# Latent norms moved into the projections, and a pair's split spread over three jobs, in a two-layer diffusion block

## The chip, the cores and the metric

The kernel runs on one core of a Trainium2 chip. A core has five engines, each with its own queue of instructions: TensorE (PE in the profile; its weight loads are a row of their own, PEld), VectorE (DVE), ScalarE (ACT), GpSimd (POOL) and SyncE (SP, which here only issues DMAs). Engines wait for each other through semaphores. Matmuls write to PSUM, in banks of 128 partitions by 512 fp32 numbers; everything else lies in SBUF. The metric is device time in microseconds for one execution, taken several times; less is better.

## What is computed

Two layers of a diffusion transformer over 512 latent tokens and 256 context tokens (768 columns in the kernel), 1024 features, all in fp32. Layer 0 runs two kinds of attention heads side by side, layer 1 another kind; both end in a SwiGLU block. The change touches the first layer's heads:

```python
def mla_heads(p_lat, p_ctx, ...):            # 8 latent-attention heads
    def queries(p, rotate):
        q = rms_norm(p[..., :256], q_norm) @ w_q_up          # query latents, 256
        ...
    def keys(p, rotate):
        c_kv = rms_norm(p[..., 256:384], kv_norm)            # key/value latent, 128
        k_rope = p[..., 384:]                                # key rope part, 32
        ...
def na_heads(q, k, v, qc, kc, vc, rel_bias, ctx_out):        # 8 neighbourhood heads
    s_lat = einsum(q, k_blk) * scale + col_bias              # keys near the query on the grid
    s_ctx = einsum(q, kc) * scale
    p = softmax(concatenate([s_ctx, s_lat], axis=-1))
    ...
def rms_norm(x, gain):
    return x * rsqrt(mean(x * x, axis=-1) + EPS) * gain
```

The two `rms_norm` of the latents are "the latent norms". The inputs of both kinds of heads come from one projection of the modulated tokens.

## The kernel before

**Arithmetic.** A product of fp32 matrices is made of three matmuls on rounded halves: with a = ah + al and b = bh + bl, the kernel adds ah·bh, ah·bl and al·bh (L324, L325, L326). So every operand must be *split*: the high half is a cast (on ACT or another engine), the low half a subtraction (on DVE or POOL). Weights are split the same way after they are loaded: wh by ACT (L311), wl by DVE or POOL (L312).

**Layer 0, projections.** Features lie on partitions, tokens along the free dimension, so that one projection gives a tile of 128 features by 768 tokens. `projections()` first makes queries and keys of the first two pairs of neighbourhood heads (head pairs 0 and 1), then goes through the string `AFTER = "012k5678"`: 0 and 1 are the two tiles of the query latents, 2 the key/value latent, k the key's rope part, 5 to 8 the raw queries and keys of pairs 2 and 3. Beside it runs background work: the modulation vectors of later stages. Their weights are loaded by DMAs that SP issues in order, multiplied on DVE and POOL (L241, L258) and summed on ACT (L259); DVE adds the parts (L261, L262). Other modulation vectors come from matmuls with the conditioning vector (L191), picked out by four small matmuls (L195).

**Layer 0, neighbourhood attention.** `na_jobs()` yields, for each of the four head pairs, three jobs (context queries, and two halves of the latent queries). A job computes scores (L768, PE, into PSUM), adds the bias and takes the running row minimum (L546, DVE; its row carries the name CUSTOM_DVE_ANT or ISA), exponentiates (L542, ACT), transposes the probabilities (L483, PE), copies and splits them out of PSUM (L474 DVE, L475 ACT), and weighs the values (L536, PE). The bias of a latent score tile is a pair of tiles loaded per head (`nb_tiles`, tag nb, two buffers).

**Side work.** Work that the attention does not need at once is put into a queue of generators, `side_work`, which `attend` advances by `step()` while it emits a job. `STEPS[0]` says how many steps a job of each pair takes, `PATTERN` at which four places of a job. `ORDER = ("2", "n3", "m", "")` says what is queued at each pair: during pair 0 the split of pair 2, during pair 1 the latent norms and the split of pair 3, during pair 2 the preparation of the latent attention (`mla_prepare`). Side work is emitted at a lower priority (`LOWER`). The order on each engine is then set by a scheduler that simulates the engines' times and takes the ready instruction of highest priority.

**What the change touches.** `split_pair` (its casts and subtractions stand at L723, L735, L744) moves a pair's raw queries and keys into split halves; `RK` says which engine casts the keys' high halves of pairs 2 and 3 (0 ACT, 1 POOL, 2 DVE). `gained` is the latent norms: squares on POOL (L962), their sum on DVE (L966), 12 column sums by matmuls with ones on PE (L969), two roots on ACT (L972, with a load of the table that holds the root, and afterwards another of the table that holds the exponential), reciprocals (L973), then a step later the transposes that spread the results over the partitions (L453), ACT's copy of them out of PSUM (L981), the multiplication by gain and root on DVE (L984) and the split (L348, L349). `latent_operands` puts the rope part of the keys into the operand of the first two latent heads by four copies (L1101), two for each. `mla_prepare` loads and splits three weights, their low halves on POOL (L312).

**PSUM.** The general ring `PG()` hands out banks by the string "stsdtsd" (tags s, t, d), one place further at each call; `PQ()` always hands out a d bank.

## Time and profile before

| what | before |
|---|---|
| time, median of 3 runs (least to most) | 1573.08 us (1572.73 to 1574.07) |
| time of the profiled execution | 1573.01 us |
| its span, first to last instruction | 1571.2 us |
| mean granted TensorE clock | 0.992 of full |
| PE busy | 1524.4 us, 97% |
| DVE busy | 1180.6 us, 75% |
| ACT busy | 804.4 us, 51% |
| POOL busy | 282.3 us, 18% |

The profiled execution is as long as the runs; 1.8 us of it lie outside the span. The busy shares are averages over many stages. The edited work lies between 100 and 262 us from the span's start: the projections end at 185, the neighbourhood attention follows. In the rows below, a line starts with L and the line's number, then come engine and operation (or engine first, in a timeline), what is written and read, the tile's size and how often. Numbers of buffers are left out of names: `pss`, `pst`, `psd` are PSUM banks with tag s, t, d; `b`, `p`, `st`, `nb`, `wr`, `wh`, `wl`, `sm` are SBUF tiles by tag. In a row of a timeline the number behind the start is a duration, and [0.67 <-ACT p L193] says that the engine sat idle for 0.67 us before it until ACT at L193 had written p.

### The profile page before, as it was taken

How to read it: one execution, taken by the hardware profiler on the slowest of the kernel's cores; microseconds unless marked ns; L12 is line 12 of the kernel's file. 1: busy time of each engine (PE TensorE's matmuls, PEld its weight loads, DVE VectorE, ACT ScalarE, POOL GpSimd, SP SyncE). 2: the span in 40 equal slices, each digit the busy share in tenths (PEclk: the TensorE clock that was granted, in tenths of full speed). 3: DMA queues.
4: the chain of work that ended last, by engine and by line, in shares of the span. 5: the costliest groups of instructions: out<-in, count | busy, mean ns of one | idle time of the engine just before them, and what ended most of it. 6: DMA issues, size and time to landing. Idle time of an engine off the chain costs nothing.

```text
span 1571.2 us, 26600 instructions
## 1 busy us (share of the span) xinstructions
PE 1524.4 (97%) x9942; PEld 1355.7 (86%) x9942; DVE 1180.6 (75%) x2351; ACT 804.4 (51%) x1638; POOL 282.3 (18%) x316
## 2 busy tenths in 40 slices
PE   6999889999999999999999999999999999999998
PEld 4787767887998999999999999877789998899997
DVE  5494878657588588895877776888877778688686
ACT  5354587777376234242433345557866445354453
POOL 0173724233010010111112110382002000000000
PEclk9999999999999999999999999999999999999999
DMA  9457242102462465656566665130016133233232
GB/s 343 153 170 235 77 132 76 44 11 95 164 224 88 148 207 174 224 156 241 179 214 245 205 242 194 40 117 32 1 29 187 45 103 130 89 100 124 86 101 88
DMA packets 82129, 216.63 MB, mean 138 GB/s; under 512 B 10832, under 2 KB 18896, under 8 KB 82000
## 3 DMA queue, kind: packets, MB, share of 16 engines
q1 hardware_dynamic: 66640, 163.02, 32.4%
q0 software_dynamic: 13056, 48.77, 9.1%
q10 hardware_dynamic: 2304, 3.15, 0.5%
q8 instruction: 78, 1.28, 0.3%
q14 instruction: 51, 0.42, 0.1%
HBM read 187.10 MB, written 23.07 MB: 134 GB/s over the span
## 4 chain that ended last, share of the span: by engine, by line
PE 74%; DVE 6%; issue 4%; DMA 3%; ACT 2%; POOL 0%; DVEq 0%; POOLq 0%; ACTq 0%; SPq 0%
PE pso L536 5%; PE pss L1408 4%; PE pss L1406 4%; PE pss L1407 4%; PE pss L324 3%; PE pss L325 3%; PE psd L324 3%; PE pss L326 3%; PE psd L1408 3%; PE psd L325 3%; PE psd L1406 3%; PE psd L326 3%; PE psd L1407 3%; PE pss L768 3%; PE pst L483 2%
## 5 line engine op out<-in xcount | busy, mean ns | idle before, releaser
L311 ACT CAST wh<-wr 128x512 fp32r<-128x512 f32 (+2 forms) x139 | 105.9, 776 | 197.4 <-DMA wr<-in_w_dn_dram 39.9
L312 DVE TENSOR_TENSOR wl<-wr,wh 128x512 fp32r<-128x512 f32 (+2 forms) x136 | 127.5, 944 | 71.2 <-ACT wh L311 70.6
L542 ACT ACTIVATE p<-p,sm 128x512 f32<-128x512 f32 (+3 forms) x144 | 105.1, 730 | 34.0 <-DVE sm L546 33.3
L1408 PE MATMUL pss<-b,wl 128*128 128x384 f32 (+1 forms) x302 | 93.8, 311 | 1.9 <-DVE wl L1394 1.9
L1406 PE MATMUL pss<-b,wh 128*128 128x384 f32 (+1 forms) x302 | 93.6, 310 | 0.0
L1407 PE MATMUL pss<-b,wh 128*128 128x384 f32 (+1 forms) x302 | 93.5, 310 | 0.0
L536 PE MATMUL pso<-ph,b 128*64 128x256 f32 (+1 forms) x400 | 78.3, 354 | 2.3 <-DVE ph L474 2.1
L1406 PE MATMUL psd<-b,wh 128*128 128x384 f32 (+1 forms) x256 | 79.8, 312 | 0.6 <-ACT p L1456 0.6
L1407 PE MATMUL psd<-b,wh 128*128 128x384 f32 (+1 forms) x256 | 79.8, 312 | 0.0
L1408 PE MATMUL psd<-b,wl 128*128 128x384 f32 (+1 forms) x256 | 79.2, 311 | 0.0
L325 PE MATMUL psd<-b,wh 128*128 128x512 f32 (+3 forms) x224 | 78.4, 350 | 0.0
L536 PE MATMUL pso<-pl,b 128*64 128x256 f32 (+1 forms) x400 | 77.7, 353 | 0.2 <-ACT pl L475 0.2
L768 PE MATMUL pss<-st,st 128*128 128x512 f32 (+2 forms) x264 | 69.8, 379 | 7.8 <-DVE sm L546 7.6
L324 PE MATMUL pss<-st,wh 128*128 128x256 f32 (+2 forms) x226 | 75.5, 334 | 0.6 <-ACT st L1393 0.6
L326 PE MATMUL pss<-st,wl 128*128 128x256 f32 (+2 forms) x226 | 75.4, 334 | 0.0
L324 PE MATMUL psd<-b,wh 128*128 128x512 f32 (+3 forms) x208 | 74.9, 360 | 0.1
L326 PE MATMUL psd<-b,wl 128*128 128x512 f32 (+3 forms) x208 | 73.4, 354 | 0.0
L325 PE MATMUL pss<-b,wh 128*128 128x256 f32 (+3 forms) x223 | 70.5, 318 | 0.0
L1393 ACT CAST wh<-ph 128x512 fp32r<-128x512 f32 x80 | 46.4, 620 | 33.4 <-DVE ph L1428 14.3
L1393 ACT CAST wh<-pl 128x512 fp32r<-128x512 f32 x80 | 45.9, 619 | 30.0 <-PE psd L1407 12.2
L1393 ACT CAST wh<-wr 128x1024 fp32r<-128x1024 f32 x40 | 42.0, 1050 | 37.0 <-PE pst L325 10.1
L483 PE MATMUL pst<-ident_r,p 128*128 128x128 f32 x346 | 58.2, 277 | 1.7 <-DVE ph L474 0.6
(615 smaller groups left out, 5315.5 us busy)
## 6 DMA issues: line engine op xcount, KB each, us to landing
wr<-in_w_gu_dram SPq DMA_DIRECT2D x88, 512.0 KB, 4.1
wr<-in_w_out_dram SPq DMA_DIRECT2D x32, 512.0 KB, 3.5
wr<-in_w_dn_dram SPq DMA_DIRECT2D x64, 256.0 KB, 2.8
p<-home SPq DMA_DIRECT2D x40, 384.0 KB, 5.0
home<-p POOLq DMA_DIRECT2D x40, 384.0 KB, 5.2
nb<-in_mod_w_dram POOLq DMA_DIRECT2D x48, 256.0 KB, 3.9
rope<-in_mod_w_dram POOLq DMA_DIRECT2D x24, 512.0 KB, 4.1
wr<-in_w_in_dram SPq DMA_DIRECT2D x21, 512.0 KB, 4.9
```

The source lines that it names most:

```text
L311: S.copy(h, r)
L312: (G if eng else V).tensor_tensor(lo, r, f(h), op=ALU.subtract)
L324: PE.matmul(o, wh[:, k], mh[:, c], start=first and k == 0, stop=False)
L325: PE.matmul(o, wh[:, k], ml[:, c], start=False, stop=False)
L326: PE.matmul(o, wl[:, k], mh[:, c], start=False, stop=last and k == n - 1)
L536: ins = PE.matmul(o[64 * i : 64 * i + 64, c], v(kt), t, start=n == 0, stop=n == len(moving[i]) - 1)
L542: S.activation(p[:, c], p[:, c], AF.Exp, bias=nm, scale=-1.0, accum_out=dn)
L768: PE.matmul(o, x, k, start=i == 0, stop=i == 1)
L1393: S.copy(h, t)
L1406: PE.matmul(o, wh, xh, start=first and k == 0, stop=False, skip_group_check=not first)
L1407: PE.matmul(o, wh, xl, start=False, stop=False, skip_group_check=not first)
L1408: PE.matmul(o, wl, xh, start=False, stop=k == 3, skip_group_check=not first)
```

## The change

The latent norms are cut in three. `latent_squares` is called inside the projections, right behind the second and third latent tile: ACT squares them, DVE adds the two of the query latents; the results go into tiles of tags nb and p. `latent_roots` is called behind projection "5": the ones-matmuls into a bank of the general ring, both roots at once, the reciprocal into a tile that stays, `latent_cols`. Behind projection "7" ACT computes one exponential whose value nobody uses, so that the exponential's table is loaded there. What is left of `gained` spreads `latent_cols` over partitions by transposes, and DVE multiplies straight out of PSUM, in pieces of 512 and 256 columns; ACT's copies and the tile they wrote are gone. The keys' high halves of pair 2 are cast by ACT instead of DVE. `STEPS[0][0]` goes from 2 to 1, so that the split of pair 2 takes one step a job. The four rope copies of `latent_operands` go from DVE to POOL. Since the roots take a bank of the general ring, all later users of it get the next place of the string.

```diff
--- before.py
+++ after.py
@@ -61,7 +61,8 @@
 C1 = 0
 VP = 0
 TURN1, MANY = (0,), 0
-RK, RQ, RL, SQ = (2, 0), (0, 0), (0, 0), 1
+RK, RQ, RL = (0,0), (0, 0), (0, 0)
+ROOTS_AT, EXP_AT = '5', '7'
 PT = (("p", "p", "p", "wr"), ("p", "p", "p", "wr"), ("p",))
 COPY = ("vva", "vvva", "vva")
 L3 = 50
@@ -72,7 +73,7 @@
 PATTERN = ("fbsfbsfbbsfs",) * 3
 BG = ((0, 0, 0, 0, 0), (2, 3), (0, 0), (0, 0))
 FIRST = 2000
-STEPS = ((2, 3, 4, 4), 5, 3)
+STEPS = ((1,3,4,4), 5, 3)
 HALVES = (slice(0, 256), slice(256, 512))
 SWAP8 = [(i // 16) * 16 + (i % 16 + 8) % 16 for i in range(32)]
 SWAP16 = [(i + 16) % 32 for i in range(32)]
@@ -949,41 +950,39 @@
 
         return use
 
-    def gained(groups):
-
-        d, m = PQ(), NT // P
-        n = m * len(groups)
-        col = T("sm", [P, 6, 2]).rearrange("p a b -> p (a b)")[:, :n]
-        for i, (tiles, _) in enumerate(groups):
-            acc = None
-            for t in tiles:
-                s = B()
-                if SQ:
-                    G.tensor_tensor(s, t, t, op=ALU.mult)
-                else:
-                    S.activation(s, t, AF.Square)
-                if acc is not None:
-                    V.tensor_tensor(s, s, acc, op=ALU.add)
-                acc = s
+    latent_cols = T("latent_cols", [P, 12])
+
+    def latent_squares(tiles, tag):
+
+        ss = [B(tag=tag) for _ in tiles]
+        for s, t in zip(ss, tiles):
+            S.activation(s, t, AF.Square)
+        for s in ss[1:]:
+            V.tensor_tensor(ss[0], ss[0], s, op=ALU.add)
+        return ss[0]
+
+    def latent_roots(accs):
+
+        d, m = PG(), NT // P
+        for i, (acc, _) in enumerate(accs):
             for j in range(m):
                 PE.matmul(d[:, i * m + j : i * m + j + 1], acc[:, j * P : (j + 1) * P], ones[:, :1], start=True, stop=True)
-        for i, (tiles, _) in enumerate(groups):
+        for i, (_, n) in enumerate(accs):
             c = slice(i * m, i * m + m)
-            S.activation(col[:, c], d[:, c], AF.Sqrt, bias=eps, scale=1.0 / (P * len(tiles)))
-        V.reciprocal(col, col)
-        yield
+            S.activation(latent_cols[:, c], d[:, c], AF.Sqrt, bias=eps, scale=1.0 / (P * n))
+        V.reciprocal(latent_cols, latent_cols)
+
+    def gained(groups):
+
+        m = NT // P
         for i, (tiles, g0) in enumerate(groups):
-            r = B()
             for c in (LATS, CTXS):
                 d, n = PQ(), (c.stop - c.start) // P
                 x = i * m + c.start // P
-                spread(d, [col[:, y : y + 1].to_broadcast([P, P]) for y in range(x, x + n)])
-                S.copy(r[:, c], d[:, : n * P])
-            res = []
-            for j, t in enumerate(tiles):
-                V.scalar_tensor_tensor(t, t, gains[:, g0 + j : g0 + j + 1], r, op0=ALU.mult, op1=ALU.mult)
-                res.append(split(t, V))
-            groups[i] = res
+                spread(d, [latent_cols[:, y : y + 1].to_broadcast([P, P]) for y in range(x, x + n)])
+                for j, t in enumerate(tiles):
+                    V.scalar_tensor_tensor(t[:, c], t[:, c], gains[:, g0 + j : g0 + j + 1], d[:, : n * P], op0=ALU.mult, op1=ALU.mult)
+            groups[i] = [split(t, V) for t in tiles]
             yield
 
     quarters = T("quarters", [P, 32])
@@ -1001,10 +1000,15 @@
         for p in range(2):
             yield from project_shifted(I["w_in0"][p], put_q(sets[p][0]), scale=0.125)
             yield from project_shifted(I["w_in0"][p + 4], put_k(sets[p][1], KC[0]))
+        accs = [None, None]
         for x in AFTER:
             if x in "012":
                 lat_raw[int(x)] = B()
                 yield from project_shifted(I["w_in0"][8 + int(x)], put(lat_raw[int(x)]))
+                if x == "1":
+                    accs[1] = latent_squares(lat_raw[:2], "nb"), 2
+                elif x == "2":
+                    accs[0] = latent_squares(lat_raw[2:], "p"), 1
             elif x == "k":
                 kr.append(B())
                 yield from project_quarters(I["w_kr"], put_rope(kr[0], rope0, SWAP8, 32, tag="p"))
@@ -1012,6 +1016,10 @@
                 raws.append(B(tag="p"))
                 i = int(x) - 5
                 yield from project_shifted(I["w_in0"][(2, 6, 3, 7)[i]], put(raws[i]), scale=(0.125, None)[i % 2])
+            if x == ROOTS_AT:
+                latent_roots(accs)
+            if x == EXP_AT:
+                S.activation(T("sm", [P, 6, 2])[:, :1, 0], latent_cols[:, :1], AF.Exp, scale=0.0)
 
     def split_pair(p):
 
@@ -1098,7 +1106,7 @@
                 (V if "z" in EV else G).memset(f(t[:32]), 0.0)
             if p == 0:
                 for i in range(2):
-                    V.tensor_copy(KA[s][i][ROPE[s]], KR[i][:32])
+                    G.tensor_copy(KA[s][i][ROPE[s]], KR[i][:32])
         (ka, kc), (qa, qb) = KA[s], QA[s][p % 2]
         for x, (hi, lo) in ((kn[p], (ka, kc)), (qn[p], (qa, qb))):
             S.copy(hi[r], x[r])
```

Lines of the changed kernel stand 1 to 8 further than those of the kernel before: L972 keeps its number by chance, L542 becomes L543, L546 becomes L547, L744 L745, L735 L736, L723 L724, L259 L260, L312 L313, L1101 L1109, L1129 L1137.

Three places show how the engines' orders move. **ACT at the start of the attention, before:** the root with its two table loads, among the exponentials (L542) of pair 0.

```order
L475 COPY ph_2106<-psd_2101 128x512
L542 ACTIVATE p_2109,sm_2074<-p_2109,sm_2075 128x256
L542 ACTIVATE p_2229,sm_2074<-p_2229,sm_2075 128x512
L972 ACT_TABLE_LOAD
L972 ACTIVATE sm_2133<-psd_2132,eps_90 128x6 x2
L542 ACT_TABLE_LOAD
L542 ACTIVATE wr_2249,sm_2074<-wr_2249,sm_2075 128x512
```

ACT in the projections, now: both loads stand among the sums of modulation parts (L260) and what moves projections out of PSUM (L437).

```order
L437 ACTIVATE p_1538<-pss_1590,sm_1587 128x512
L260 ACTIVATE pl_1582,part_1606<-pl_1582 128x512
L972 ACT_TABLE_LOAD
L972 ACTIVATE latent_cols_740<-pst_1633,eps_90 128x6 x2
L260 ACTIVATE ph_1623,part_1675<-ph_1623 128x512
```

And some ten rows later the exponential:

```order
L437 ACTIVATE p_1649<-psd_1692,sm_1689 128x512
L260 ACTIVATE pl_1759,part_1779<-pl_1759 128x512
L828 COPY sm_1784<-pst_1742 128x2
L1022 ACT_TABLE_LOAD
L1022 ACTIVATE sm_1822<-latent_cols_740 128x1
L437 ACTIVATE p_1735<-pst_1742,sm_1784 128x256
```

The attention's start holds no table load any more.

**DVE from the projections' end to the first scores, before:** the last modulation vector, pair 2's key split (casts L744, low halves L735), then the first minimum (L546).

```order
L262 SCALAR_TENSOR_TENSOR mod_305_1447<-mod_305_1447,modb_84 128x1
L744 CAST b_1949<-p_1625 64x768
L735 TENSOR_TENSOR b_1950<-p_1625,b_1949 64x768
L744 CAST b_1951<-p_1625 64x768
L735 TENSOR_TENSOR b_1952<-p_1625,b_1951 64x768
L546 ISA p_1928,sm_1918<-pss_1927,zeros_94 128x256
```

Now:

```order
L263 SCALAR_TENSOR_TENSOR mod_308_1453<-mod_308_1453,modb_84 128x1
L200 SCALAR_TENSOR_TENSOR mod_399_1909<-pss_1929,modb_84 128x2
L200 SCALAR_TENSOR_TENSOR mod_400_1910<-pss_1929,modb_84 128x2
L547 ISA p_1954,sm_1944<-pss_1953,zeros_94 128x256
```

The split is gone from here; two small vectors that wait for the picking matmuls (L195 before, now ahead of the first scores on PE) stand in its place. The key split's casts are on ACT, some 35 rows into the attention (L745 there), each with its L736 on DVE behind it.

**POOL from the attention's start to the weights of `mla_prepare`, before:** value copies (L1129), low halves of pair 2's queries (L723), the squares (L962), low halves of pair 3, then low halves of weights (L312).

```order
L723 TENSOR_TENSOR b_1947<-p_1530,b_1947 64x768
L723 TENSOR_TENSOR b_1948<-p_1530,b_1948 64x768
L962 TENSOR_TENSOR b_2134<-b_1314 128x768
L962 TENSOR_TENSOR b_2142<-b_1115 128x768
L962 TENSOR_TENSOR b_2144<-b_1210 128x768
L723 TENSOR_TENSOR st_2236<-p_1711,st_2236 64x768
L723 TENSOR_TENSOR st_2237<-p_1711,st_2237 64x768
L312 TENSOR_TENSOR wl_2391<-wr_2388,wh_2390 128x1024
L312 TENSOR_TENSOR wl_2397<-wr_2394,wh_2396 128x512
```

Now:

```order
L724 TENSOR_TENSOR b_1973<-p_1538,b_1973 64x768
L724 TENSOR_TENSOR b_1974<-p_1538,b_1974 64x768
L724 TENSOR_TENSOR st_2205<-p_1735,st_2205 64x768
L724 TENSOR_TENSOR st_2206<-p_1735,st_2206 64x768
L1137 COPY b_2347<-b_702 64x384 x2
L1137 COPY b_2347<-b_703 64x384 x2
L313 TENSOR_TENSOR wl_2390<-wr_2387,wh_2389 128x1024
L1109 COPY st_2632<-b_2405 32x768
L1109 COPY st_2633<-b_2406 32x768
L313 TENSOR_TENSOR wl_2396<-wr_2393,wh_2395 128x512
L313 TENSOR_TENSOR wl_2402<-wr_2399,wh_2401 128x1024
```

The squares are gone, and two of the rope copies (L1109) now stand ahead of the low halves of the two query weights; they read what DVE's split of the rope key writes.

## The prediction, made before the changed kernel was run

> **What bounds the kernel now.** I read the page first, the busy shares of parts 1 and 2, to see which engine can carry time at all.
>
> ```profile
> span 1571.2 us, 26600 instructions
> PE 1524.4 (97%) x9942; PEld 1355.7 (86%) x9942; DVE 1180.6 (75%) x2351; ACT 804.4 (51%) x1638; POOL 282.3 (18%) x316
> ```
>
> The profiled execution took 1573.01 us, 1.8 more than its span; the median of the three runs shown is 1573.08, so the sum below, made against 1573.0, stands for both. PE is busy 97% of the span: only the rest, and stretches at a reduced clock, can be won. A difference of 0.2% (3.1 us) is about what a measurement of this kernel can tell from none. Next I read busy time by stage around the edited place: the end of layer 0's projections, the start of the neighbourhood attention, and what follows.
>
> ```profile
> core 0: us, PE busy (x) PEld busy (x) DVE busy (x) ACT busy (x) POOL busy (x), PEclk, DMA share, GB/s
> 100.00:185.00 85.00, 85.00 (x547) 67.09 (x549) 61.45 (x117) 41.06 (x99) 47.23 (x45) 1.00 0.57 167
> 185.00:191.70 6.70, 2.79 (x26) 1.57 (x22) 6.43 (x7) 3.46 (x5) 6.51 (x5) 0.79 0.39 88
> 191.70:198.00 6.30, 6.17 (x28) 5.04 (x28) 3.42 (x14) 4.32 (x14) 3.69 (x3) 0.68 0.35 95
> 198.00:216.20 18.20, 16.56 (x132) 12.70 (x132) 14.22 (x39) 15.90 (x36) 3.63 (x2) 1.00 0.50 131
> 216.20:230.00 13.80, 11.38 (x46) 6.47 (x44) 9.56 (x21) 11.91 (x29) 2.65 (x1) 0.75 0.43 144
> 230.00:252.00 22.00, 19.18 (x145) 14.95 (x144) 19.84 (x33) 16.18 (x37) 14.46 (x11) 1.00 0.32 96
> 252.00:290.00 38.00, 37.02 (x280) 29.80 (x279) 28.81 (x81) 28.20 (x68) 10.49 (x11) 1.00 0.27 75
> 290.00:400.00 110.00, 108.88 (x816) 87.88 (x817) 71.61 (x200) 77.50 (x176) 37.05 (x27) 1.00 0.18 64
> ```
>
> The first number is the stretch's length, then come the busy times, and after POOL the granted clock. Up to 185 PE is never idle while ACT sits idle for 44 of 85 us: whatever PE gets there costs its full length, whatever ACT gets there costs nothing unless someone waits for it. From 185 to 252 PE is idle for 10.9 us (length less busy, summed over five rows), and two rows show a low clock, 0.68 and 0.75. In the last row PE is busy 99%, so a gain ahead of it passes to the end almost whole. Who keeps PE waiting stands in its timeline (start, length, and in brackets the idle time ahead and what ended it):
>
> ```profile
> 184.55 0.40 PE L326 MATMUL psd<-b,wl 128*128 128x512 f32 x1
> 185.87 0.73 PE L768 MATMUL pss<-st,st 128*128 128x256 f32 x4
> 187.28 0.61 PE L195 MATMUL pst<-pick,p 128*128 128x2 f32 x4 [0.67 <-ACT p L193]
> 191.73 1.22 PE L768 MATMUL pss<-st,st 128*128 128x256 f32 x4 [3.27 <-DVE sm L546]
> 203.64 1.58 PE L768 MATMUL pss<-st,st 128*128 128x256 f32 x6 [1.25 <-DVE sm L546]
> 220.92 1.35 PE L768 MATMUL pss<-b,b 128*128 128x256 f32 x4 [0.80 <-DVE sm L546]
> 236.49 0.73 PE L768 MATMUL pss<-b,b 128*128 128x512 f32 x2 [1.11 <-DVE sm L546]
> 240.48 0.32 PE L536 MATMUL pso<-ph,b 128*64 128x128 f32 x1 [1.18 <-DVE ph L474]
> ```
>
> The first two rows are the projections' last matmul and the first scores. After that DVE ends nearly every wait: L546 adds the bias and takes the row minimum of a score tile, which frees its bank. The longest wait, 3.27, is late because DVE had other work in front:
>
> ```profile
> 184.60 0.87 DVE L744 CAST b<-p 64x768 fp32r<-64x768 f32 x1
> 185.57 1.07 DVE L735 TENSOR_TENSOR b<-p,b 64x768 fp32r<-64x768 f32 x1
> 186.67 2.06 DVE L744 CAST b<-p 64x768 fp32r<-64x768 f32 x1
> 188.83 2.37 DVE L735 TENSOR_TENSOR b<-p,b 64x768 fp32r<-64x768 f32 x1
> 191.24 0.42 DVE L546 CUSTOM_DVE_ANT_0 p<-pss,zeros 128x256 f32<-128x256 f32 x1
> ```
>
> That is the K half of pair 2's split, and it fills DVE until 191.20.
>
> **The change part by part.** The groups of 185 to 262 price what is removed or moved (count, busy us and mean ns of one, idle time ahead):
>
> ```profile
> L1101 DVE CAST st<-b 32x768 fp32r<-32x768 f32 x4 | 7.2, 1811 | 0.1
> L744 DVE CAST b<-p 64x768 fp32r<-64x768 f32 x2 | 2.9, 1467 | 0.0
> L966 DVE TENSOR_TENSOR b<-b,b 128x768 f32<-128x768 f32 x1 | 0.9, 947 | 0.0
> L542 ACT ACT_TABLE_LOAD x2 | 2.6, 1283 | 0.0
> L972 ACT ACT_TABLE_LOAD x1 | 1.3, 1283 | 0.0
> L981 ACT COPY b<-psd 128x512 f32<-128x512 f32 x2 | 1.1, 565 | 0.0
> L981 ACT COPY b<-psd 128x256 f32<-128x256 f32 x2 | 0.7, 370 | 0.0
> L348 ACT CAST b<-b 128x768 fp32r<-128x768 f32 x3 | 2.5, 833 | 0.0
> L744 ACT CAST st<-p 64x768 fp32r<-64x768 f32 x2 | 1.7, 830 | 0.0
> L1129 POOL COPY b<-b 64x384 f32<-64x384 f32 x6 | 5.0, 826 | 0.3
> L969 PE MATMUL psd<-ones,b 128*128 128x1 f32 x24 | 2.9, 236 | 0.0
> ```
>
> *Squares, roots, table into the projections.* Three squares of 128x768 on ACT, 0.83 each by L348 of the same width, two table loads of 1.28, one DVE add of 0.95: all lie in idle time of ACT (44 us) and DVE (23.5 us) and cost nothing; without that cover they would cost 2.5+2.6+0.95, about 6 us. The 24 ones-matmuls are different. They come from the attention, where PE has slack, into the stage where it has none: +2.9 there, −2.9 between 198 and 216. The new wait is that of the roots' matmuls for squares and add; these are emitted three projections earlier, so I price it at nothing; if the squares were late, PE's queue would stand behind them, with the whole projections waiting. The dummy exponential is one column of 128x1, in the same idle time. SP's queue gets one more wait: the first head's bias tiles share their buffers with the squares and are loaded among modulation weights, the second once the roots are done. Three projections follow the roots; one has 8x3x2 = 48 matmuls, at 85.0/547 each 7.5 us, so some 22 us lie between this load and the attention, whose bias it is. Modulation weights queued behind it have DMA shares of 0.57 around them; I price it at nothing, a few us if SP stood still for longer.
>
> *185 to 191.7.* The projections end about 2.6 later (between a group's 2.9 and somewhat less, since the matmuls overlap). But the L744 and L735 of pair 2 leave this place (K's casts go to ACT, the split is one step a job, so its K half comes a job later). The first L546 then waits for PE alone: scores follow the modulation sums, 185.87−184.95 after the projections' end, and the pick matmuls of 0.6 with their wait of 0.67 now stand before them: 187.6+0.9+1.3+0.6 = 190.4 against 191.24. Gain 0.8. From below: if the scores wait for something else, −2.6; from above: the whole 3.27.
>
> *191.7 to 198.* PE does 6.17 us of work at a clock of 0.68; at full clock that is 4.2, and ACT's 4.32 becomes the longer. The slow stretch follows the one long wait, which is gone, so I take 1.8 (bounds 0 and 2.0).
>
> *198 to 216.2.* PE falls by 2.9 to 13.7. ACT loses the Sqrt load, one reload of the exponential's table and 0.4 of roots (−3.0) and gains two casts of 0.83: 14.6. DVE loses the add and the reciprocal (−1.2), gains the two L735 (+1.9): 14.9. The longest is 14.9 instead of ACT's 15.9, and of the 2.3 us that the stretch is longer than ACT's work, the 1.25 wait at 203.64 should go in part. I take 2.0 (0 if chains of short waits stay, 3.3 if DVE's 14.9 binds alone).
>
> *216.2 to 230.* Here the four ACT copies vanish (−1.8), because DVE now reads the spread rows from PSUM. DVE's three L984 become six halves:
>
> ```profile
> L984 DVE SCALAR_TENSOR_TENSOR b<-b,mla_gain,b 128x768 f32<-128x768 f32 x3 | 4.3, 1445 | 0.7 <-ACT b L981 0.7
> ```
>
> The same columns, one wait (0.7) fewer. But PE's clock is 0.75 here without any long idle time, which I cannot explain from the rows: 0.5 if it stays, 1.9 if it goes. I take 1.2.
>
> *230 to 252.* DVE is busy 19.84 of 22.0 and loses four L1101, 7.2 us in all. Two of them stand in front of the waits at 236.49 and 240.48 (1.11+1.18). Gain 2.0; bounds 0 and PE's idle 2.8.
>
> *The key-rope copies on POOL.* What stands behind them is the low half of a query weight, whose first reader on PE comes at 243.45:
>
> ```profile
> 233.98 0.94 DVE L349 TENSOR_TENSOR b<-b,b 32x768 fp32r<-32x768 f32 x1
> 236.90 2.40 POOL L312 TENSOR_TENSOR wl<-wr,wh 128x1024 fp32r<-128x1024 f32 x1 [0.83 <-ACT wh L311]
> 243.45 0.47 PE L326 MATMUL psd<-b,wl 128*128 128x512 f32 x1
> ```
>
> The copies wait for DVE's split (over at 234.92). POOL shows no such copy; by L1129, 0.826 for 384 columns, one of 768 is estimated at 1.65. Two of them and the splits of 1.29 (the 128x512 one) and 2.40: 234.92+3.3+1.3+2.4 = 241.9, 2.6 later than 239.3, inside the 4.15 us of slack. The low halves that POOL makes for the next head come later too. I take −1.0 (0 to −3).
>
> POOL's work has a price on DVE too: L744 took 0.87 before POOL's subtraction started, and 2.06 beside it.
>
> ```profile
> 185.80 4.59 POOL L723 TENSOR_TENSOR b<-p,b 64x768 fp32r<-64x768 f32 x2
> ```
>
> [...]
>
> *Sum.* 0.8+1.8+2.0+1.2+2.0−1.0 = 6.8, so 1573.0−6.8 = **1566.2**. Behind 252 the bank order of the ring turns by one and a few matmuls change places at 99% load: ±1.5, taken as nothing. The floor: all idle time of 185 to 252 (10.9) and both clock losses (6.17×0.32+11.38×0.25 = 4.8) make 15.7, so 1557.3.
>
> **The rivals.**
>
> *Moved, not saved (also: it doesn't do what it says).* The ones-matmuls cost PE 2.6 where it is full; ACT, at 15.9 of 18.2, gets two casts; the slow clock comes a few us later, since scores still start with waits. For it: the low clock at 216 to 230 without a long wait. Against: DVE's queue before the first L546 is the plain cause of 3.27. Only the 2.0 of 230 to 252 would be left: 1571.0.
>
> *Both slow stretches vanish.* If a low clock follows from PE's sparse work anywhere before it, an unbroken start keeps the clock up throughout: 1.8 becomes 2.0, the stretch 216 to 230 gives 11.38×0.25 = 2.8 with the 0.8 wait in place of 1.2, the copies cost nothing, and the 1.25 wait goes whole. 0.8+2.0+3.3+3.6+2.0 = 11.7, 1561.3. Against it: the second stretch has no wait over 0.8 ahead of it.
>
> [...]
>
> *POOL becomes the bound (slower).* Place: POOL at 235 to 245. If DVE and POOL stretch each other (L744's 2.06 for 0.87; the two L735 1.07 and 2.37), a copy takes 1.65×2.3 = 3.8, the weight's low half ends at 234.92+7.6+3.7 = 246.2, 2.8 past its reader's turn, and the second head's copies the same again: PE idles some 5.6, at 0.75 clock behind it another 4 of 16 us. With the rest of the gain reduced by DVE's own blocking to 5.5 or so, the balance is 1573.0+5.6+4−5.5 = 1577.1. It decides from 4.15 us of lateness on. Against: the readers of the weight stand later in PE's order now, which adds slack.
>
> **How the numbers follow.** My forecast 0.54, moved-not-saved 0.17, both stretches 0.17, POOL 0.12. The forecast's own range is 1562.5 to 1569. The first rival lies within 0.2%, the second below it, the last above: faster 0.71, same 0.17, slower 0.12. A range of 1558.5 to 1574.0 holds the first three less the floor's edge and leaves out the slower case.
>
> **What would show it.** Right: first L546 near 190.4 with no L744 of DVE ahead and no wait of 3 us on PE; clock 1.00 from 190 to 198; no table load between 187 and 262; L984 reading PSUM; PE's idle time of 185 to 252 down from 10.9 to 5 or 6. Wrong: projections over 3 us longer or with a gap (squares late); L326 waiting for POOL near 243; low clock elsewhere in 200 to 260; or the loss of a gain behind 290, where only the bank order differs.

## The result, and the profile after

The changed kernel takes 1561.99 us (median of 4 runs, 1560.35 to 1564.28) against 1572.9 of the kernel before (4 runs). The ratio is 0.994, with a 95% interval from 0.9925 to 0.9954: about 9.4 us faster (7 to 12). The forecast was 1566.2, the range 1558.5 to 1574.0. The profiled execution has a span of 1559.6 us, 11.6 less than before. Busy time by the same stretches of the clock as in the prediction (length, busy times, and after POOL the granted clock; the projections now last until 188.8, so that the first row still holds some of them):

```profile
185.00:191.70 6.70, 6.21 (x43) 4.40 (x41) 1.13 (x7) 3.69 (x8) 5.51 (x6) 1.00 0.00 0
191.70:198.00 6.30, 5.88 (x38) 4.25 (x36) 4.18 (x15) 4.63 (x14) 0.00 (x0) 1.00 0.21 66
198.00:216.20 18.20, 15.46 (x116) 11.57 (x116) 16.86 (x43) 15.76 (x37) 6.28 (x6) 1.00 0.72 173
216.20:230.00 13.80, 12.54 (x92) 9.01 (x90) 13.34 (x34) 13.04 (x34) 4.17 (x4) 1.00 0.58 179
230.00:252.00 22.00, 21.50 (x162) 17.76 (x162) 14.36 (x42) 18.36 (x46) 12.08 (x9) 1.00 0.32 93
252.00:290.00 38.00, 38.00 (x299) 30.98 (x295) 27.45 (x78) 28.19 (x63) 16.74 (x15) 1.00 0.26 70
```

Between 185 and 252 PE now idles for 5.4 us, 10.9 before, and the clock stays at 1.00 in every row; both slow stretches are gone. PE's longest waits there (its timeline, brackets as before):

```profile
198.35 1.34 PE L769 MATMUL pss<-st,st 128*128 128x512 f32 x4 [0.61 <-DVE sm L547]
201.64 0.33 PE L484 MATMUL pst<-ident_r,p 128*128 128x128 f32 x1 [0.92 <-ACT p L543]
217.07 0.63 PE L484 MATMUL psd<-ident_r,p 128*128 128x128 f32 x4 [0.61 <-DVE b L984]
224.76 0.44 PE L484 MATMUL psd<-ident_r,p 128*128 128x128 f32 x2 [0.65 <-ACT p L543]
```

None reaches a microsecond; before there were four of 1.1 to 3.3. Where the time went shows when the same instruction is looked up in both traces (L546 is taken as the n-th of its kind; the orders differ, so that single values can be off by up to 3 us):

| place (time before) | after | shift |
|---|---|---|
| first projection matmul, 75.58 | 76.86 | +1.3 |
| last projection matmul, 184.55 | 188.41 | +3.9 |
| first L546, 191.24 | 191.28 | 0.0 |
| L546 of 198.3 | 197.6 | −0.7 |
| L546 of 216.1 | 214.9 | −1.2 |
| L546 of 247.1 | 238.8 | −8.3 |
| L546 of 257.2 | 246.4 | −10.8 |
| L546 of 290.5 | 279.4 | −11.1 |
| end of the span, 1571.2 | 1559.6 | −11.6 |

The first 1.3 lie ahead of everything edited; the same place lies between 0.5 earlier and 1.9 later in the traces of the experiments below that leave it alone, so this is spread between executions. Without it the projections end 2.6 later, as forecast, and the path up to 216 wins some 2.5. The gain itself comes between 216 and 257; behind 290 nothing more is won or lost.

PE's own account says where the time lay. From the projections' last matmul to the L546 of 290.5 it takes 105.6 us before (184.95 to 290.51) and 90.6 now (188.81 to 279.44), 14.9 less. PE idles 6.5 less in it (11.9 and 5.4); the 24 ones-matmuls of 2.9 have left it; and before, PE did 3.97 and 6.31 us of work in two stretches at half rate (granted clock 0.50, 188.9 to 195.7 and 223.0 to 229.9), half of which, 5.1, is the price of the rate. Together these are 14.5. This is an account of PE's time and not yet a cause: what was saved at one place may be waited away at the next.

Two chains of waits (start, length, what) show what bounded 210 to 250. The kernel before, a selection:

```profile
213.07 1.28 ACT L972
214.36 0.43 ACT sm L972 x2
...
218.72 0.48 ACT b L981
219.25 0.88 PE psd L453 x6
...
223.18 1.04 ACT wh L311
...
224.72 0.48 ACT b L981
225.24 1.11 PE psd L483 x4
226.36 1.05 PE pso L536 x2
...
234.95 0.75 DVE st L1101
...
237.67 2.03 DVE st L1101
...
247.82 4.39 DVE st L1101 x2
```

Root, copies out of PSUM, transposes at half rate, then the rope copies. The changed kernel's chain has none of these; from the projections' end to 240 its longest pieces are five loads of bias tiles, three of them behind 210:

```profile
194.37 3.20 DMA nb<-in_nb_dram
...
198.94 3.09 DMA nb<-in_nb_dram
...
210.83 3.45 DMA nb<-in_nb_dram
...
228.97 3.80 DMA nb<-in_nb_dram
...
234.27 3.13 DMA nb<-in_nb_dram
```

### The profile page after: what moved, and what is told of

Read it like the earlier page. It is cut to its first block, busy times and chain, and to the rows that moved or that the text cites. A ratio compares the mean times of both kernels' runs of the same rounds, so it can differ in the third digit from the quotient of the medians.

```text
span 1559.6 us, 26600 instructions
## 1 busy us (share of the span) xinstructions
PE 1521.7 (98%) x9942; PEld 1355.6 (87%) x9942; DVE 1172.4 (75%) x2348; ACT 805.4 (52%) x1639; POOL 281.4 (18%) x317
## 3 DMA queue, kind: packets, MB, share of 16 engines
q8 instruction: 78, 1.28, 0.4%
## 4 chain that ended last, share of the span: by engine, by line
PE 88%; DVE 6%; DMA 4%; issue 1%; ACT 1%; SPq 0%; DVEq 0%; ACTq 0%
PE pso L537 5%; PE pss L1416 4%; PE psd L325 4%; PE pss L325 4%; PE pss L1415 4%; PE pss L1414 4%; PE pss L326 4%; PE psd L326 4%; PE pss L327 4%; PE psd L327 4%; PE psd L1416 3%; PE psd L1415 3%; PE psd L1414 3%; PE pst L1414 3%; PE pst L1416 3%; PE pst L1415 3%
## 5 line engine op out<-in xcount | busy, mean ns | idle before, releaser
L312 ACT CAST wh<-wr 128x512 fp32r<-128x512 f32 (+2 forms) x139 | 106.0, 777 | 196.7 <-PE pss L326 37.5
L313 DVE TENSOR_TENSOR wl<-wr,wh 128x512 fp32r<-128x512 f32 (+2 forms) x136 | 126.5, 936 | 69.9 <-ACT wh L312 69.1
L543 ACT ACTIVATE p<-p,sm 128x512 f32<-128x512 f32 (+3 forms) x144 | 104.9, 729 | 29.9 <-DVE sm L547 29.2
L326 PE MATMUL psd<-b,wh 128*128 128x512 f32 (+3 forms) x253 | 86.2, 341 | 0.0
L325 PE MATMUL psd<-b,wh 128*128 128x512 f32 (+3 forms) x213 | 75.8, 357 | 0.2 <-DVE b L475 0.2
L325 PE MATMUL pss<-st,wh 128*128 128x512 f32 (+2 forms) x212 | 71.9, 339 | 0.0
L327 PE MATMUL pss<-st,wl 128*128 128x512 f32 (+2 forms) x212 | 71.8, 339 | 0.0
L1416 PE MATMUL psd<-b,wl 128*128 128x384 f32 (+1 forms) x226 | 70.8, 313 | 0.4 <-DVE wl L1402 0.4
L1415 PE MATMUL psd<-b,wh 128*128 128x384 f32 (+1 forms) x226 | 70.7, 313 | 0.0
L1414 PE MATMUL psd<-b,wh 128*128 128x384 f32 (+1 forms) x226 | 70.5, 312 | 0.0
L1401 ACT CAST wh<-wr 128x1024 fp32r<-128x1024 f32 x40 | 42.1, 1053 | 39.2 <-PE pss L326 10.1
```

Source lines behind the costliest of these rows:

```text
L312: S.copy(h, r)
L313: (G if eng else V).tensor_tensor(lo, r, f(h), op=ALU.subtract)
L325: PE.matmul(o, wh[:, k], mh[:, c], start=first and k == 0, stop=False)
L326: PE.matmul(o, wh[:, k], ml[:, c], start=False, stop=False)
L327: PE.matmul(o, wl[:, k], mh[:, c], start=False, stop=last and k == n - 1)
L543: S.activation(p[:, c], p[:, c], AF.Exp, bias=nm, scale=-1.0, accum_out=dn)
```

## The experiments

Names beginning with b are the kernel before with something added, names beginning with a are the changed kernel with something taken back. Ratios are to the kernel before, run on the same chip in the same rounds; microseconds are the ratio's distance from 1, or from the changed kernel's 0.994, times 1570.5. The changed kernel's own interval reaches 2.3 us to either side, so the last column is no finer than that; a_roots_back's interval overlaps it, and a_copy's only just does not.

| kernel | ratio | 95% interval | against before | against the change |
|---|---|---|---|---|
| changed kernel | 0.9940 | 0.9925 to 0.9954 | −9.4 | |
| b_norms | 1.0002 | 0.9992 to 1.0012 | +0.3 | +9.7 |
| b_split | 1.0010 | 1.0002 to 1.0019 | +1.6 | +11.0 |
| b_rope_pool | 0.9995 | 0.9986 to 1.0004 | −0.8 | +8.6 |
| b_ring | 1.0001 | 0.9992 to 1.0009 | +0.2 | |
| a_rope_dve (norms + split) | 0.9941 | 0.9928 to 0.9955 | −9.3 | +0.2 |
| a_split_back (norms + rope) | 0.9980 | 0.9972 to 0.9988 | −3.1 | +6.3 |
| b_rope_split (rope + split) | 0.9978 | 0.9967 to 0.9989 | −3.5 | +6.0 |
| a_roots_back | 0.9958 | 0.9942 to 0.9974 | −6.6 | +2.8 |
| a_rk_back | 0.9981 | 0.9971 to 0.9991 | −3.0 | +6.4 |
| a_copy | 0.9967 | 0.9955 to 0.9979 | −5.2 | +4.2 |
| b_fill | 1.0007 | 0.9998 to 1.0016 | +1.1 | |
| a_one_bias | 0.9931 | 0.9918 to 0.9945 | −10.8 | −1.4 |

### One part alone

**b_norms**: the changed kernel with split and rope copies as before.

```diff
-RK, RQ, RL = (0,0), (0, 0), (0, 0)
+RK, RQ, RL = (2, 0), (0, 0), (0, 0)
-STEPS = ((1,3,4,4), 5, 3)
+STEPS = ((2, 3, 4, 4), 5, 3)
-                    G.tensor_copy(KA[s][i][ROPE[s]], KR[i][:32])
+                    V.tensor_copy(KA[s][i][ROPE[s]], KR[i][:32])
```

> The kernel before with the latent norms' part of the change alone (squares by ScalarE, roots and both table loads within the projections, VectorE reading the spread rows from PSUM); key split on VectorE at two steps a job and rope copies on VectorE as before. Theory 1, the sum of the prediction (many small terms): roots out of 198 to 216 and the copies out of 216 to 230 give 2.0+1.2, against the 2.6 later end of the projections: about 1570 to 1572, 1 to 3 us gained. Theory 2 (the norms' burst): between 213 and 231 the two table loads, the roots, the spreads and their copies hold up ScalarE, two PSUM banks and with them TensorE, and that is where most of the 11 us lie: 7 to 10 us gained, about 1564. Theory 3 (VectorE's queue, rope copies first): under 3 us gained.

Measured: no change (1571.53 against 1570.65). Theory 2 falls, and theory 1's 1 to 3 us are not there either.

**b_split**: the kernel before with the two numbers of the split.

```diff
-RK, RQ, RL, SQ = (2, 0), (0, 0), (0, 0), 1
+RK, RQ, RL, SQ = (0, 0), (0, 0), (0, 0), 1
-STEPS = ((2, 3, 4, 4), 5, 3)
+STEPS = ((1, 3, 4, 4), 5, 3)
```

> The kernel before with pair 2's split alone changed (keys' high halves cast by ScalarE, one step a job). Theory 1: the wait of 3.27 before the second scores and the low clock of 191 to 198 go, 0.8+1.8 plus the 2.6 that the projections are not longer here, less ScalarE's two added casts (1.7): 3 to 5 us gained, about 1569. Theory 2: what is won at 191 is lost again at 213 to 231, where ScalarE and the norms bind: within 2 us of before. Theory 3: as theory 1 or less.

Measured: 1.6 us slower. The wait of 3.27 is gone, and in its trace the first L546 starts 3.3 earlier than before; but the row of the norms is much as it was, and slow stretches stand at 225 and 239:

```profile
216.20:230.00 13.80, 9.42 (x45) 5.53 (x44) 9.33 (x18) 12.83 (x30) 2.43 (x2) 0.88 0.41 134
230.00:252.00 22.00, 18.60 (x122) 14.15 (x121) 16.29 (x32) 14.14 (x34) 8.03 (x7) 0.84 0.27 83
```

PE is busy for 9.42 of 13.8, 4.4 us idle. What is won at 191 is waited away 30 us later.

**b_rope_pool**: the kernel before with the four copies on GpSimd.

```diff
-                    V.tensor_copy(KA[s][i][ROPE[s]], KR[i][:32])
+                    G.tensor_copy(KA[s][i][ROPE[s]], KR[i][:32])
```

> The kernel before with the four rope copies alone on GpSimd. Theory 1: 2.0 gained less 1.0 for GpSimd: about 1572. Theory 2: 0 to 2 us gained. Theory 3: 4 to 8 us gained, since VectorE is the busiest engine of 230 to 252: about 1567.

Measured: −0.8, not to be told from none. Theory 3 falls.

**b_ring**: the kernel before with the bank ring moved on by one.

```diff
+            if x == "5":
+                ring[0] += 1
```

> The kernel before, in which nothing but the general ring of PSUM banks is advanced by one place behind projection 5, as the change does by taking a bank for the roots. All three theories: no change beyond 1.5 us either way. A fourth one: the shifted order of banks, not the moved work, brings a good part of the gain: 4 us or more.

Measured: no change. The shifted order of banks brings nothing, here or behind 290.

So three parts worth 0.3, 1.6 and −0.8 alone are worth −9.4 together. The theories that hang the gain on one part fall; the next question is which parts need each other.

### One part left out

**a_rope_dve**: the changed kernel, rope copies back on VectorE.

```diff
-                    G.tensor_copy(KA[s][i][ROPE[s]], KR[i][:32])
+                    V.tensor_copy(KA[s][i][ROPE[s]], KR[i][:32])
```

> The changed kernel with the four rope copies back on VectorE, all else as changed (norms and split). No part alone had moved the time by over 0.1%. Theory A (the parts fill each other's gaps: TensorE's idle time and its half-rate windows go only when no gap is left anywhere between 185 and 260): each part left out brings back a good share, here 3 to 7 us of the 11. Theory B (norms and split belong together, the rope copies are a trifle): within 1.5 us of the changed kernel. Theory C (the gain hangs on rope copies and norms, both off VectorE at 216 to 250): 7 us or more come back.

Measured: the same time as the changed kernel. Theory B is right on this one. But why do copies that stood in the chain with 7.2 us not matter? They are not the same size any more. First the four copies in the kernel before, then in this one (min/median/max of the duration in ns, first and last start):

```profile
L1101 DVE CAST st<-b x4: 753/2120/2251, 234.9 to 250.0; 32x768 fp32r<-32x768 f32 x4
```

```profile
L1109 DVE CAST st<-b x4: 544/550/1335, 228.4 to 240.7; 32x768 fp32r<-32x768 f32 x4
```

Before, the last two ran from 247.82 to 252.2 while POOL was at work; the rows of POOL in the kernel before:

```profile
246.48 1.83 POOL L1105 TENSOR_TENSOR st<-b,st 64x768 fp32r<-64x768 f32 x1 [4.31 <-ACT st L1104]
248.25 1.41 POOL L1098 MEMSET st<- 32x768 f32 x2
249.74 2.06 POOL L1105 TENSOR_TENSOR st<-b,st 64x768 fp32r<-64x768 f32 x1
```

In a_rope_dve POOL is idle from 237.7 to 241.4, where its last two copies lie, and they take 0.55 each. In these two traces the copy took 0.55 with POOL idle and up to 2.25 with POOL at work. So the price of this part is not fixed: it depends on what POOL does at that moment, which the other parts move.

**a_split_back**: the changed kernel, pair 2's split as before (RK and STEPS as in the diff of b_norms).

> The changed kernel with pair 2's split as before (keys' high halves cast by VectorE, two steps in the first job), norms and rope copies as changed. Theory A: 3 to 7 us of the 11 come back. Theory B: 8 us or more come back, since norms without the split gained nothing. Theory C: under 3 us come back.

Measured: 6.3 come back, theory A. **b_rope_split**: the kernel before with the edits of b_split and b_rope_pool.

> The kernel before with rope copies and split as changed, and the latent norms as before. Theory A: 3 to 7 us of the 11 are kept. Theory B: nothing is kept, 0 to 2 us gained. Theory C: nothing is kept, 0 to 2 us gained. In A the trace shows one half-rate stretch in place of two, in B and C two.

Measured: 3.5 kept, theory A, though not in the form expected: its trace has two slow stretches, each half as long as those before. Of its chain of waits, where the norms stand as before:

```profile
215.24 1.28 ACT L972
216.54 0.42 ACT sm L972 x2
216.98 1.28 ACT L542
...
220.77 0.47 ACT b L981
...
225.59 0.48 ACT b L981
226.11 0.66 PE psd L483 x4
```

Both table loads are pieces of the path, 2.56 us, and PE's transposes wait behind the copy. Rope copies and split together win 3.5, rope copies beside the norms 3.4 (b_norms against a_split_back), beside norms and split nothing.

With these, all eight combinations of the three parts have been measured, and PE's idle time from 185 to 290 can be set beside the times: 11.9 us before, 13.0 with the norms alone, 12.5 with the split alone, 9.5 with the rope copies alone, 9.0 and 9.1 with norms or split beside the rope copies, 5.5 with norms and split, 5.4 with all three. Only norms and split together bring it to half, and with it the time.

**a_roots_back**: squares in the projections, but matmuls, roots and both table loads back in the attention.

```diff
-        d, m = PG(), NT // P
+        d, m = PQ(), NT // P
     def gained(groups):
 
         m = NT // P
+        latent_roots(accs)
+        yield
...
-                    accs[1] = latent_squares(lat_raw[:2], "nb"), 2
+                    accs[1] = latent_squares(lat_raw[:2], "b"), 2
-                    accs[0] = latent_squares(lat_raw[2:], "p"), 1
+                    accs[0] = latent_squares(lat_raw[2:], "b"), 1
...
-            if x == ROOTS_AT:
-                latent_roots(accs)
-            if x == EXP_AT:
-                S.activation(T("sm", [P, 6, 2])[:, :1, 0], latent_cols[:, :1], AF.Exp, scale=0.0)
```

> The changed kernel with squares in the projections, but the ones-matmuls, the roots, their table load and the exponential's reload back in the attention (through a d bank, as before); spreads read from PSUM, split and rope copies as changed. If the loads and roots on ScalarE between 205 and 220 are what makes the gap there: 4 us or more come back, and a half-rate stretch with them. If it is the order of the split and the copies alone: under 2 us come back, and 2 to 3 are won in the projections, which end earlier by the matmuls' time.

Measured: 2.8 come back, not clear of noise, with a slow stretch at 210; between the two answers expected. The projections end at 186.27, 2.1 earlier than in the changed kernel, and the attention is longer by more than that.

**a_rk_back**: only the keys' high halves back on VectorE, one step a job as changed.

```diff
-RK, RQ, RL = (0,0), (0, 0), (0, 0)
+RK, RQ, RL = (2, 0), (0, 0), (0, 0)
```

> The changed kernel with the keys' high halves of pair 2 back on VectorE, but still one step a job, so that they come after the first scores. The split as a whole was worth 6 us beside norms and rope copies. If what counts is that it no longer stands ahead of the first minimum on VectorE (its place): within 1.5 us of the changed kernel. If what counts is VectorE's load (two casts of 0.87 to 2.06 more): 3 to 6 us come back.

Measured: 6.4 come back, as much as without the whole split. So it is not the place ahead of the first minimum; that place is free here. Of the two answers expected VectorE's load is left, and the rows show how it costs: DVE's, POOL's beside them, and PE's:

```profile
201.10 0.55 DVE L745 CAST b<-p 64x768 fp32r<-64x768 f32 x1
202.18 2.34 DVE L736 TENSOR_TENSOR b<-p,b 64x768 fp32r<-64x768 f32 x1
204.55 2.06 DVE L745 CAST b<-p 64x768 fp32r<-64x768 f32 x1
206.64 0.69 DVE L547 CUSTOM_DVE_ANT_0 wr<-pss,nb 128x512 f32<-128x512 f32 x1
```

```profile
201.88 4.30 POOL L724 TENSOR_TENSOR st<-p,st 64x768 fp32r<-64x768 f32 x2 [10.73 <-ACT st L723]
```

```profile
207.39 2.17 PE L769 MATMUL pss<-st,st 128*128 128x256 f32 x6 [3.11 <-DVE sm L547]
```

The cast of 0.55 takes 2.06 and the subtraction of 0.95 takes 2.34 while POOL subtracts, and PE waits 3.11 for the minimum behind them. The delay passes on to the bias loads: the one that left SP at 203.49 in the changed kernel leaves at 207.97 here, in both 0.03 us after the end of an L547 that read a bias tile. So it waits for DVE, and not for the split's own DMAs ahead of it in SP's queue. This trace is 8.0 us longer than the changed kernel's; 2.8 of that arise at these rows, and 1.3 ahead of them at a bias load that took 4.47 instead of 3.20 (more on it under a_copy).

**a_copy**: ScalarE copies the spread rows out of PSUM again.

```diff
+            r = B()
             for c in (LATS, CTXS):
...
-                for j, t in enumerate(tiles):
-                    V.scalar_tensor_tensor(t[:, c], t[:, c], gains[:, g0 + j : g0 + j + 1], d[:, : n * P], op0=ALU.mult, op1=ALU.mult)
-            groups[i] = [split(t, V) for t in tiles]
+                S.copy(r[:, c], d[:, : n * P])
+            res = []
+            for j, t in enumerate(tiles):
+                V.scalar_tensor_tensor(t, t, gains[:, g0 + j : g0 + j + 1], r, op0=ALU.mult, op1=ALU.mult)
+                res.append(split(t, V))
+            groups[i] = res
```

> The changed kernel with the spread rows copied out of PSUM by ScalarE again (four copies, 1.8 us) and VectorE multiplying from SBUF in pieces of 768 columns, all else as changed. By the prediction's sum 0.5 to 1.9 us come back. If the copies are one link of the burst that opens the gaps on TensorE: 3 us or more, and a half-rate stretch after 210. If only roots and split matter: under 0.5 us.

Measured: 4.2 come back, with slow stretches at 200.8 and 224.7. The copies are four instructions of 1.8 us, and ACT is not even busy there:

```profile
216.20:230.00 13.80, 9.98 (x47) 6.03 (x44) 9.22 (x23) 10.10 (x24) 0.00 (x0) 0.88 0.41 135
```

ACT 10.1, DVE 9.2, PE 10.0 of 13.8: no engine is full, each waits for another. It would be natural to say that a spread's bank is held until ACT gets to the copy, and that this delays the rest. The trace does not show it. Its chain of waits from 190 to 230 has no copy and no multiplication in it, but late bias loads (chain, then DVE's timeline):

```profile
194.94 4.55 DMA nb<-in_nb_dram
...
212.41 5.48 DMA nb<-in_nb_dram
```

```profile
217.92 0.69 DVE L547 CUSTOM_DVE_ANT_1 wr<-pss,nb 128x512 f32<-128x512 f32 x1 [3.23 <-DMA nb<-in_nb_dram]
```

In the changed kernel the same two loads start at 194.37 and 210.83 and take 3.20 and 3.45. So 3.4 of the 7.0 us by which this trace is longer than the changed kernel's are slow loads, and the first of them lies ahead of every copy. The first load behind the projections took 4.4 to 4.6 us in b_norms, a_split_back, a_rk_back and a_copy and 3.0 to 3.2 in all other traces that have it. What made it slow in these four was not tested. The 4.2 is therefore no clean price of the copies.

### The clock, and what bounds the changed kernel

**b_fill**: the kernel before, with 20 matmuls that nobody reads put around PE's wait of 3.27 (18 ran from 185.30 to 189.88, two at 191.25).

```diff
                     front = front and next(j)
+                    if fillers and phase[0] == 0:
+                        fillers.pop()()
...
+    def filler():
+        for _ in range(2):
+            d = PQ()
+            for _ in range(10):
+                PE.matmul(d, ident_r, sets[0][0][0][:, :512], start=True, stop=True)
+
+    fillers.append(filler)
```

> The kernel before with 20 matmuls of 128x512 whose result nobody reads (into d banks, about 0.21 us each, 4 us in all), put on TensorE between the first scores and the second ones, where it waits 3.27 us for VectorE; no other work is moved. Theory A1 (the half rate follows a stretch of 3.4 us in which TensorE is busy for less than about half): the clock stays at 1.00 from 188.9 to 195.7, the 6.17 us of work of that stretch take 4.2, and 1 to 2.5 us are gained though work was added; the stretch at 223 may stay. Theory A2 (the half rate comes from something else, such as the load on the other engines or chance): the stretch stays and the time is unchanged or up to 2 us longer.

Measured: the slow stretch goes, the time does not.

```profile
185.00:191.70 6.70, 6.01 (x34) 5.06 (x31) 6.42 (x10) 3.39 (x7) 6.55 (x4) 1.00 0.42 95
191.70:198.00 6.30, 5.69 (x38) 4.21 (x37) 4.00 (x13) 4.11 (x13) 2.87 (x3) 1.00 0.32 90
```

The clock is 1.00 where it was 0.79 and 0.68, and the ratio is 1.0007 (0.9998 to 1.0016). From the projections' last matmul to the 13th L546 it takes 19.3 us, 19.6 before. So at this place the half rate went with PE's idle time, as theory A1 has it, though A1's "less than about half" is not shown: PE was busy for 2.30 of the 3.41 us ahead of 188.9. And it cost next to nothing here: the work waits at either rate for DVE and then for a bias load, as DVE's timeline shows for the kernel before and for this one:

```profile
202.88 0.69 DVE L546 CUSTOM_DVE_ANT_0 wr<-pss,nb 128x512 f32<-128x512 f32 x1 [2.04 <-DMA nb<-in_nb_dram]
```

```profile
201.72 0.69 DVE L546 CUSTOM_DVE_ANT_0 wr<-pss,nb 128x512 f32<-128x512 f32 x1 [2.05 <-DMA nb<-in_nb_dram]
```

The second stretch, at 223, stayed in this kernel and its price was not measured by itself; it lies on the chain of waits of the kernel before (225.24 and 226.36 above), so that one can have cost more, up to half of its 6.31 us of work.

Over all runs the half rate does not order the times. From 185 to 290 b_norms, b_fill, b_rope_split, a_rk_back and a_copy each have 6.8 us of it, at +0.3, +1.1, −3.5, −3.0 and −5.2 us. But the changed kernel, a_rope_dve and a_one_bias, the three fastest, have none there, so that a share of the clock in the gain is not excluded.

**a_one_bias**: the changed kernel with two bias tiles for all heads, loaded once.

```diff
+    one_bias = []
+
     def nb_tiles(h):
-        ts = [T("nb", [P, NT]) for i in range(2)]
-        for i in range(2):
-            dma(ts[i], I["nb"][h, i])
+        if not one_bias:
+            one_bias.extend(T("nb", [P, NT]) for i in range(2))
+            for i in range(2):
+                dma(one_bias[i], I["nb"][h, i])
+        ts = one_bias
```

> The changed kernel, in which the two bias tiles of the first head are loaded once and used by all eight neighbourhood heads: 14 of 16 bias loads are left out, so the attention's result is another one; all other work stays. In the changed kernel's chain of waits between 200 and 240 four loads of bias tiles stand with 3.1 to 3.8 us each (21.7% of 200 to 262), each of which begins when VectorE has read the tile two places earlier. Theory N (these loads are what now bounds the neighbourhood attention; in the kernel before they were covered by the longer stalls of VectorE and ScalarE): TensorE's idle time of 185 to 290 (5.4 us) falls to under 3 and 2 to 5 us are gained on the changed kernel. Theory O (the loads are late, but TensorE has other work meanwhile and is bound by its own 98%): under 1 us gained.

Measured: 1.4 us less than the changed kernel, with intervals that overlap; PE idles 5.0 us from 185 to 290, 5.4 in the changed kernel. Theory O is the nearer. The loads are the last thing in the chain, but taking them away hardly helps, because PE is now nearly full in this stage (21.50 of 22.0, 38.00 of 38.0). This kernel does less than the reference asks for and is no version to keep; no run here beats the changed kernel clear of noise.

## Why the prediction was right, and where its steps failed

The direction held and the time lies in the range; the sum did not hold in its terms: 6.8 forecast, 9.4 measured by the ratio, 11.6 between the two profiles. Against the two traces the terms between 191.7 and 216 were 2.6 too large and those behind 216 some 7.7 too small. That the sum came as near as it did is in part luck, since errors of opposite sign offset each other.

- **Projections 2.6 later**: 2.6, once the 1.3 that both executions' starts differ by are taken off. Over all traces the projections take 111.6 to 113.2 us with the ones-matmuls and 108.5 to 111.5 without, so the agreement to 0.1 is chance, the size is not. Squares and both table loads cost nothing there, as forecast: ACT's rows in the changed kernel's projections are 0.83 to 0.85 and 1.28 each, and PE shows no gap for the roots.
- **185 to 191.7, 0.8**: the first L546 was to start at 190.4; it started at 191.28, which is 190.0 without the 1.3. Right.
- **191.7 to 198, 1.8**: the shift grows by 0.7. The step that failed is "at full clock that is 4.2": b_fill gives this stretch its full clock and the path wins 0.3. The half rate was a sign of the wait and next to no price of its own here.
- **198 to 216.2, 2.0**: 0.5. The wait of 1.25 at 203.64 was to go in part with the work taken off DVE and ACT. It fell to 0.50, but the L546 that ends it had itself waited 2.04 for a bias load (202.88 above), and in the changed kernel it still waits 1.03 for it. And the longest of the busy sums was taken as the length; DVE has 16.86 there now instead of the 14.9 worked out, because the norms' multiplications (L984) have moved up into this stretch. What is done earlier here no longer stands in DVE's queue later.
- **216.2 to 252, 1.2+2.0−1.0**: 7.1 by the L546 of 247.1 and 9.9 by that of 290.5. This is the term that was mis-sized. Its working failed where the prices were added, each against the rest of the kernel before. They don't add: the same rope copies are worth 0.8 alone, 3.4 beside the norms and 0.2 beside norms and split. The 1.2 was also a middle between a second slow stretch that stays and one that goes; it went. The price of the copies out of PSUM, at most 1.9, is not refuted: a_copy's 4.2 are not all theirs.
- **The rope copies on GpSimd, −1.0**: nothing. A copy there takes 0.82, half the 1.65 estimated from a 64x384 one, and no matmul waits for the weight's low half:

```profile
L1109 POOL CAST st<-b 32x768 fp32r<-32x768 f32 x4 | 3.2, 820 | 1.1 <-DVE b L350 0.9
```

- **What was left out**: the bias loads of the later heads, 3 us and more each, which start when DVE has read an earlier tile. The prediction looked at the first head's tiles only.
- **Two smaller slips**: the 0.87 of L744 was taken as its price without POOL, but POOL was copying just then (L1129, 183.43 to 185.83); with POOL idle a cast of this size took 0.55 (a_rk_back, 201.10). And the floor leaves out the clock loss of 185 to 191.7, 2.79×0.21 = 0.6.

Of the rivals, "both slow stretches vanish" gave 1561.3, nearer to the measured 1562.0 than the forecast, and its sign is in the trace: the clock is 1.00 from 185 to 290. It made the clock the cause. For the first stretch b_fill speaks against that; for the second, up to 3.2 us, no run decides. "Moved, not saved" did come true for the split alone (+1.6) and for the norms alone (+0.3), each of which the prediction had put at a gain. "POOL becomes the bound" did not come: DVE's casts did get longer beside POOL, as it assumed (2.06 against 0.55 in a_rk_back, where POOL's two L724 beside them took 4.30, 3.76 in the changed kernel), but the rope copies took 0.82 on POOL and nobody waited for them.

What explains the size, as far as the runs go: from 185 to 260 the kernel before has three sources of delay on in-order queues (key casts, and POOL where it works beside them; root, loads and copies of the norms; rope copies beside POOL). Either of the first two that is left keeps PE waiting, so neither is worth its price alone; with both gone PE is nearly full, and the third no longer counts. That norms and split need each other is shown by the eight combinations. That the in-order queues are the link is read from the traces, best at the casts of a_rk_back (the cast of 204.55 ends at 206.61, the minimum behind it starts at 206.64). How the 9.4 divide between the links, and what share the second slow stretch has, is not settled.

## What to carry to other kernels

When a stage has several delays in parallel, price an edit against the kernel that the other edits leave, and try them together before dropping one: three parts that did nothing alone gave 0.6% together. When one part is taken back, look in the trace whether the time comes back at that part: in a_copy's trace half of it stood at bias loads. A load that waits for its buffer belongs in the sum of a stage like any other step. The low granted clock behind the projections was a sign of PE's idle time: in b_fill junk in that time brought the clock from 0.79 and 0.68 to 1.00, and the time stayed.

## What the runs showed of the hardware

- **Up to 290 us the kernel before has half-rate stretches of 3.4 us or twice that, and PE was at work for more than half of the time just ahead of two of them.** The granted clock was 0.50 from 21.6 to 25.1, from 188.9 to 195.7 and from 223.0 to 229.9; the first of these is 3.41 us long, and 223.0 − 188.9 is ten times 3.41. In the 3.41 us just ahead of the two later ones PE was busy for 2.30 and 1.96 us, and 3.41 us with 2.14 had no stretch behind them (the first three rows, kernel before). In b_norms a stretch followed 0.81 (its clock from 252 to 290 is 0.96), none followed 1.59:

```profile
185.49:188.90 3.41, 2.30 (x22) 1.28 (x10) 3.20 (x3) 2.99 (x4) 3.33 (x3) 1.00 0.51 115
219.62:223.03 3.41, 1.96 (x10) 1.08 (x9) 2.58 (x7) 2.67 (x7) 0.00 (x0) 1.00 0.75 261
202.55:205.96 3.41, 2.14 (x12) 1.49 (x14) 3.08 (x9) 3.39 (x8) 2.08 (x2) 1.00 0.75 192
```

```profile
200.42:203.83 3.41, 1.59 (x11) 0.68 (x11) 1.64 (x6) 1.02 (x3) 0.00 (x0) 1.00 0.03 9
251.62:255.03 3.41, 0.81 (x6) 0.81 (x7) 3.20 (x7) 0.86 (x3) 1.35 (x1) 1.00 0.00 0
```

  So PE's busy time in the 3.41 us ahead does not divide the two kinds: 2.30 stands on one side, 1.59 and 2.14 on the other. What decides is not shown.
- **Beside POOL's work DVE's casts and subtractions took 1.1 to 4.1 times as long as with POOL idle.** The cast of 32x768: 0.55 with POOL idle (a_rope_dve, L1109), 0.75 to 2.25 in the kernel before (L1101). The cast of 64x768: 0.55 with POOL idle (a_rk_back, 201.10), 0.87 beside POOL's copies (kernel before, 184.60), 2.06 beside its subtractions (kernel before, 186.67; a_rk_back, 204.55). The subtraction of 64x768: 0.95 with POOL idle (a_rk_back, 209.52), 1.07 where POOL went from copies to its subtractions (kernel before, 185.57), 1.25 beside POOL's copies (changed kernel, 205.27), 2.34 and 2.37 beside its subtractions (a_rk_back, 202.18; kernel before, 188.83).
